# The last value block of two FFN parts, computed by feature instead of by token

## The chip, the core and the metric

The kernel runs on one core of a Trainium2 chip. The metric is device time in microseconds, the median over runs. An extra profiled execution leaves the trace from which every row here is quoted. Engines: PE does matmuls and PEld loads their stationary operand; DVE and ACT do elementwise work; POOL and SP here mostly issue DMAs, POOL the accumulating ones. Each engine works off its own queue in order.

## The reference

One layer of a hybrid decoder over 256 tokens of width 2048, in float32. The change lies in its last stage, the gated FFN with a causal convolution of three taps along the tokens, of inner width 5632:

```python
def conv_gated_ffn(hn, w_up, conv_w, conv_b, w_down):
    up = causal_dwconv(hn @ w_up, conv_w, conv_b)
    gate, val = jnp.split(up, 2, axis=-1)
    return (jax.nn.silu(gate) * val) @ w_down
```

`hn` is the normalised residual stream; the FFN's output is added to that stream, and a final normalisation follows.

## The kernel before

**Weights.** All weights stream through once, in 1 MiB pieces of 4 x 128 rows by 512 columns (`raw`, six buffers). For each piece ACT casts a high part (`hi`, L286) and DVE subtracts for a low part (`lo`, L287); there are three buffers of each. A matrix product in float32 accuracy is three products: high x high, low x high, high x low. A piece is a *unit* of PE work. The stream is prepared two units ahead, and the cast of a unit waits until PE has read the `hi` of the unit three before.

**FFN parts.** The 11 blocks of 512 inner columns are done in parts of 4, 4 and 3. In a part each block has a gate product and a value product with `ffn_w_up`, 22 in all, each of four units; then the part is multiplied by its rows of `ffn_w_down` into the residual.

**Two forms of an up product.** `gemm_n` (L362, L363 with the high part of the weights, L369 with the low part) computes *by token*: tokens on the partitions, 512 features along the free axis, one accumulator in PSUM. The convolution and the later products want features on the partitions, so the result is turned: `row_planes` splits the words into 16-bit planes (two ACT copies, L757, which also free the accumulator), `turn_planes` turns them with two transposing DMAs on SP (L1205, tile `d`), and after a number of units `join_planes` puts the words together again (four ACT copies, L763, tile `jp`), followed by a product on DVE with the tokens' scale `rsb` (L1271). `gemm_t` (L351) computes *by feature*: the weights are stationary, features come out on the partitions in two accumulators, the high part of the weights moving 512 columns and the low part 256. `scaled` then joins each accumulator's two halves (ACT copy L544, tile `c`; DVE addition L545, tile `uz`, which frees the accumulator) and multiplies by `rsb` (L676). There are three accumulators of this kind in all (`acc`).

Both forms end in `conv` (ACT L1281, DVE L1283, into `fg` for gate and `fv` for value) and, for a value block, `hidden`: a tanh (L1354), two products (L1355, L1356, tile `fo`), and a split into high and low part (L555, L556, tile `s`), once for each half `pr` of the block. Eight such `s` make `hid` of a part of four.

```python
def up(c0, b, at, then):
    if at is None:
        for pr, a in enumerate(gemm_t("ffn_w_up", 0, h2s, NT, c0 + b * BW)):
            then(pr, scaled(a, "uz"))
        return
    d = turn_planes(row_planes(gemm_n("ffn_w_up", 0, h2s, NT, c0 + b * BW)))
    def turned(pr):
        z = join_planes(d, pr)
        dve.tensor_tensor(out=z, in0=z, in1=rsb2, op=ALU.mult)
        then(pr, z)
    for pr in range(2):
        later(at[pr], lambda pr=pr: turned(pr))
```

`later(n, fn)` runs `fn` n + 1 units on in the program's text. A scheduler then orders each engine's queue from that text; the work of one step may be spread between others.

**The down pair.** In a part of four, `pair_add` computes two output blocks at a time with fewer products, in eleven units in this order: q1, p0, q3, p1, q5, q2, q6, p2, q7, q4, p3. A q unit is 12 matmuls, a p unit 24. Three weight pieces are held: A (of q1), B (of q3) and C (of q2). After q1, POOL's DMA adds a further piece onto A in SBUF (L267); that sum is q5. Then DVE adds B to A (L294) for q6, POOL's DMA adds a piece onto B for q7, and DVE adds C to A (L292) for q4. So q7 and q4 depend on a chain: q5's cast and remainder, A+=B, the accumulating DMA onto B (it may only start when B has been read), and the casts. Units p2 and p3 use the last two blocks' `hid`; p2 reads the two halves of the last value block in its matmuls (`s`). The pair takes three accumulators: q1 writes the first, p0 is the first to write the third, which p2 completes. Additions into the residual are L427.

In part 3, which has three blocks, the last value block goes by feature already (`at` is None), and its down products are plain `gemm_n`.

Of the kernel before, what the change touches and what calls it, by code (L numbers as in the profile page):

```python
# [20 lines left out]
NT = D // P  # L21
# [5 lines left out]
FF = 5632  # L27
NF = FF // P
BW = 512
# [125 lines left out]
def hybrid_layer(  # L155
# [34 lines left out]
    def big(shape, dt=F32, s="b"):  # L190
        return bp.tile(shape, dt, tag="big", name=nm(s))
# [4 lines left out]
    def acc():  # L196
        return pm.tile([P, 2, BW], F32, tag="acc", name=nm("acc"))
# [106 lines left out]
    def later(n, fn):  # L304

        pending.append((step[0] + n + 1, fn))
# [16 lines left out]
    def chunks(nk, w, row, c):  # L323

        for i, (kind, parts) in enumerate(units(w, row, nk, c)):
            yield i * KC, parts

    def gemm_t(w, row, st, nk, col):

        accs = [acc(), acc()]  # L330
        first = gemms[0] == 0
        phase = 0
        for k0, parts in chunks(nk, w, row, col):
            last = k0 + KC >= nk
            tiles = [(kk, j) for j in range(2) for kk in range(KC)]
            if first and k0 == 0:
                runs = [[(t, pr, kk, j) for t in (0, 1)] for pr in range(2) for kk in range(KC) for j in range(2)]
            elif last:
                runs = [[(t, pr, kk, j) for kk, j in tiles] for pr in range(2) for t in (1 - pr, pr)]
            else:  # L340
                runs = [[(t, pr, kk, j) for pr in range(2) for kk, j in tiles] for t in (phase, 1 - phase)]
                phase = 1 - phase
            for i, run in enumerate(runs):
                for t, pr, kk, j in run:
                    k = k0 + kk
                    sx = st[k // 2][:, k % 2, :]
                    part = parts[kk // KH][t][:, kk % KH, (2 * pr + j) * P : (2 * pr + j + 1) * P]
                    a = accs[pr][:, j, :]
                    if t == 1:
                        a, sx = a[:, S:BW], sx[:, 0:S]  # L350
                    pe.matmul(  # L351
                        a, part, sx, start=k == 0 and t == 0, stop=k == nk - 1 and t == 0, skip_group_check=True
                    )
                if i + 1 == len(runs) // 2 and not last:
                    st[(k0 + KC) // 2 + 1]
        return accs
# [14 lines left out]
    def gemm_n(w, row, st, nk, col):  # L371

        a = acc()
        for k0, parts in chunks(nk, w, row, col):
            ops = [
                [halves(st[(k0 + k) // 2], (k0 + k) % 2, slice(tt * P, (tt + 1) * P)) for k in range(KC)]
                for tt in range(2)
            ]
            for tt in range(2):
                upper_n(a[:, tt, :], ops[tt], parts, k0 == 0)  # L380
            for tt in range(2):
                lower_n(a[:, tt, :], ops[tt], parts, k0 + KC >= nk)
        return a
# [155 lines left out]
    def joined(a, s="j"):  # L539

        c = tmp("c")
        o = tmp(s)
        with tc.high_priority(URGENT):
            act.copy(c, a[:, :, S:BW])  # L544
            dve.tensor_tensor(out=o, in0=a[:, :, 0:S], in1=c, op=ALU.add)  # L545
        return o
# [127 lines left out]
    def scaled(a, s):  # L674
        z = joined(a, s)
        dve.tensor_tensor(out=z, in0=z, in1=rsb2, op=ALU.mult)  # L676
        return z
# [81 lines left out]
    def join_planes(d, pr):  # L759

        t = tmp("jp")
        for i in range(2):
            ins = act.copy(words(t)[:, :, :, 1 - i], d[:, i, 2 * pr : 2 * pr + 2, :])  # L763
            if i == 0:
                tc.keep_in_program_order(ins)
        return t
# [115 lines left out]
    for g in range(2):  # L882
        dec = big([P, 4, S], s="dec")
        vs, turned = [], []
        for b, o in enumerate((O_Q, O_K)):
            a = qjoin if g == b == 0 else [joined(t, "q") for t in gemm_t("w_in", 0, xs, NT, o + g * BW)]
# [298 lines left out]
    def row_planes(o):  # L1185

        t = big([P, 2, 2, BW], U16, s="rp")
        planes(t, o)
        return t
# [11 lines left out]
    def turn_planes(rows):  # L1201

        d = big([P, 2, KC, S], U16, s="d")
        for tt in range(2):
            sp.dma_start_transpose(  # L1205
                out=d.rearrange("p a c s -> p (a c) s")[:, :, tt * P : (tt + 1) * P],
                in_=rows[:, tt].rearrange("p a w -> p (a w)"),
            )
        return d
# [45 lines left out]
    h2s = []  # L1255
# [5 lines left out]
# [16 lines that stand above are left out]
    def conv(c0, b, pr, z, dst):  # L1277
        for j in range(2):
            t = c0 // P + 4 * b + 2 * pr + j
            y = dst[:, 2 * pr + j, :]  # L1280
            act.activation(y, z[:, j, :], AF.Identity, scale=pf[:, 2, t : t + 1], bias=pf[:, 3, t : t + 1])  # L1281
            for s in range(1, 3):
                dve.scalar_tensor_tensor(  # L1283
                    out=y[:, s:S], in0=z[:, j, 0 : S - s], scalar=pf[:, 2 - s, t : t + 1], in1=y[:, s:S],
                    op0=ALU.mult, op1=ALU.add,
                )
# [55 lines left out]
    def put_rows(n, bs):  # L1342
        for b in bs:
            sp.dma_start(out=fkept[n, b], in_=hrow[b])

    def get_rows(n, bs):
        for b in bs:
            hrow[b] = big([P, 2, BW], s="nat")
            sp.dma_start(out=hrow[b], in_=fkept[n, b])

    def hidden(gt, vl, pr, summed):
        cs = slice(2 * pr, 2 * pr + 2)
        th, o = tmp("ft"), tmp("fo")
        act.activation(th, gt[:, cs, :], AF.Tanh, scale=0.5)  # L1354
        dve.scalar_tensor_tensor(out=o, in0=th, scalar=1.0, in1=gt[:, cs, :], op0=ALU.add, op1=ALU.mult)  # L1355
        dve.tensor_tensor(out=o, in0=o, in1=vl[:, cs, :], op=ALU.mult)  # L1356
        hid.append(split_pair(o, 0.5))
        if summed and len(hid_sums) < KC:
            hid_sums.append(sums(o, 0.5))
# [3 lines left out]
    for part, nb_ in enumerate(FF_PARTS):  # L1363
        final = part == len(FF_PARTS) - 1
        paired = nb_ == 4
        hid, hid_sums = [], []
        for b in range(b0, b0 + nb_):
            gt, vl = big([P, 4, S], s="fg"), big([P, 4, S], s="fv")
            last = b + 1 == b0 + nb_
            up(0, b, (1, 2), lambda pr, z, b=b, gt=gt: conv(0, b, pr, z, gt))  # L1370
            if last:
                later(0, lambda part=part, n=2 if paired else 4: get_rows(part % 2, range(n)))

            def finish_up(pr, z, b=b, gt=gt, vl=vl, paired=paired):
                conv(FF, b, pr, z, vl)
                hidden(gt, vl, pr, paired)

            up(FF, b, None if last and not paired else (2, 4) if last else (1, 2), finish_up)
        if final:
            wfin = []  # L1380
            for i in range(2):
                t = big([P, 2, BW], s="wf")
                sp.dma_start(
                    out=t.rearrange("p a n -> p (a n)"),
                    in_=final_norm_w[i * 1024 : (i + 1) * 1024].partition_broadcast(P),
                )
                wfin.append(t)
        if nb_ == 4:
            for b in (0, 2):
                if b == 0:  # L1390
                    later(8, lambda part=part: get_rows(part % 2, (2, 3)))
                pair_add("ffn_w_down", b0 * BW, hid, hid_sums, b * BW, (b + 1) * BW, hrow[b], hrow[b + 1])
                put_rows((part + 1) % 2, (b, b + 1))
        else:
            for b in range(4):
                down(b0, hid, b, final)
        b0 += nb_
# [35 lines left out]
```

## Time and profile before

| | us |
|---|---|
| median of 3 runs (1996.22 to 1998.04) | 1997.41 |
| the profiled execution | 1995.6 |
| its span, first to last instruction | 1993.8 |
| PE busy | 1968.6 |
| DVE busy | 1566.4 |
| ACT busy | 1277.2 |

A row of the timeline reads: start, duration, engine, line, operation, output<-input, shape, count, and in brackets the idle time before it with what ended it. Line numbers are those of the kernel before. Matmuls overlap by design: two that are back to back start 0.227 us apart though each is listed with 0.39.

### The profile page before, as it was taken

The numbers are of one execution on the slowest core, as the hardware profiler recorded it, in microseconds if no ns is written. First come the engines' busy times: TensorE is split into PE (matmuls) and PEld (weight loads), VectorE is DVE, ScalarE is ACT, GpSimd is POOL, SyncE is SP. The second block draws the span as 40 slices with busy tenths as digits, with TensorE's granted clock in tenths as the row PEclk, the third lists the DMA queues.
The fourth block names the chain that finished last, engine by engine and source line by source line (L and its number), as shares of the span: only waits on it lengthen the run. The fifth ranks groups of instructions, "written<-read, shape, count | busy, mean of one in ns | idle before, by whom it ended". The sixth has DMA issues, their size and how long they took to land.

```text
span 1993.8 us, 23634 instructions
## 1 busy us (share of the span) xinstructions
PE 1968.6 (99%) x9304; PEld 1650.8 (83%) x9304; DVE 1566.4 (79%) x1546; ACT 1277.2 (64%) x1323; POOL 43.2 (2%) x52
## 2 busy tenths in 40 slices
PE   9999999999999999999999999999989999899998
PEld 7888888888888888888888888888878888788887
DVE  6978888889886886779988778677786777885775
ACT  6655656767677554567778756567744667546662
POOL 0000000000000000000000000000000000000000
PEclk9999999999999999999999999999999999899999
DMA  9675674655887865878998748766777677686671
GB/s 369 233 261 147 223 264 161 230 190 160 266 260 220 248 250 190 252 256 258 270 259 235 267 125 271 236 226 204 234 232 273 207 219 236 204 278 228 211 245 61
DMA packets 146463, 456.59 MB, mean 229 GB/s; under 512 B 77744, under 2 KB 82480, under 8 KB 98608
## 3 DMA queue, kind: packets, MB, share of 16 engines
q1 hardware_dynamic: 139072, 410.51, 58.7%
q0 software_dynamic: 5760, 41.95, 11.6%
q10 hardware_dynamic: 1520, 2.63, 0.4%
q8 instruction: 73, 1.20, 0.2%
q14 instruction: 38, 0.31, 0.0%
HBM read 420.96 MB, written 16.78 MB: 220 GB/s over the span
## 4 chain that ended last, share of the span: by engine, by line
PE 91%; DVE 4%; ACT 2%; DMA 1%; issue 1%; SPq 0%; POOLq 0%; ACTq 0%; DVEq 0%
PE acc L362 25%; PE acc L363 25%; PE acc L369 24%; PE acc L351 14%; PE sm L518 2%; DVE lo L287 1%; ACT hi L286 1%; DMA raw<-in_wall 1%; PE acc L518 1%; PE sm L948 1%; PE sm L532 1%; DVE raw L294 0%; DVE fv L1283 0%; DMA d<-rp 0%; DVE tb L722 0%
## 5 line engine op out<-in xcount | busy, mean ns | idle before, releaser
L287 DVE TENSOR_TENSOR lo<-raw,hi 128x2048 fp32r<-128x2048 f32 (+1 forms) x420 | 950.9, 2267 | 297.8 <-ACT hi L286 297.0
L286 ACT CAST hi<-raw 128x2048 fp32r<-128x2048 f32 (+1 forms) x418 | 793.2, 1901 | 522.7 <-PE acc L363 374.8
L362 PE MATMUL acc<-hi,s 128*128 128x512 f32 x2008 | 787.3, 392 | 12.4 <-ACT hi L286 12.3
L363 PE MATMUL acc<-hi,s 128*128 128x512 f32 x2008 | 784.3, 391 | 0.0
L369 PE MATMUL acc<-lo,s 128*128 128x512 f32 x2008 | 501.1, 389 | 0.0
L362 PEld LDWEIGHTS acc<-hi,s 128*128 128x128 f32 x2008 | 378.6, 189 | 91.5 <-ACT hi L286 13.2
L363 PEld LDWEIGHTS acc<-hi,s 128*128 128x128 f32 x2008 | 378.9, 189 | 78.5 <-DVE s L556 1.0
L369 PEld LDWEIGHTS acc<-lo,s 128*128 128x128 f32 x2008 | 377.1, 188 | 78.3
L351 PE MATMUL acc<-s,hi 128*128 128x512 f32 x832 | 200.4, 392 | 2.1 <-DVE hi L284 1.5
L351 PEld LDWEIGHTS acc<-s,hi 128*128 128x128 f32 x832 | 153.5, 188 | 32.8 <-issue 1.6
L362 PE MATMUL acc<-hi,ss 128*128 128x512 f32 x320 | 125.8, 393 | 0.8 <-ACT o L454 0.6
L363 PE MATMUL acc<-hi,ss 128*128 128x512 f32 x320 | 124.7, 390 | 0.0
L763 ACT COPY jp<-d 128x512 uint16<-128x512 uint16 x132 | 93.4, 771 | 29.4 <-DMA d<-rp 29.3
L351 PEld LDWEIGHTS acc<-s,lo 128*128 128x128 f32 x832 | 107.1, 191 | 4.9 <-DVE lo L287 1.3
L351 PE MATMUL acc<-s,lo 128*128 128x256 f32 x832 | 110.5, 284 | 0.5 <-DVE lo L287 0.5
L369 PE MATMUL acc<-lo,ss 128*128 128x512 f32 x320 | 85.6, 389 | 0.0
L362 PEld LDWEIGHTS acc<-hi,ss 128*128 128x128 f32 x320 | 60.1, 188 | 14.5 <-ACT o L454 1.4
L369 PEld LDWEIGHTS acc<-lo,ss 128*128 128x128 f32 x320 | 60.1, 188 | 12.6
L363 PEld LDWEIGHTS acc<-hi,ss 128*128 128x128 f32 x320 | 60.1, 188 | 12.2
L267 POOL DMA_DIRECT2D raw<-in_wall x40 | 35.2, 880 | 1550.7 <-DVE lo L287 887.5
L427 DVE TENSOR_TENSOR nat<-nat,acc 128x512 f32<-128x512 f32 (+1 forms) x49 | 44.0, 910 | 14.9 <-PE acc L369 14.9
L292 DVE TENSOR_TENSOR raw<-raw,raw 128x2048 f32<-128x2048 f32 x20 | 45.8, 2288 | 0.4
(235 smaller groups left out, 1251.7 us busy)
## 6 DMA issues: line engine op xcount, KB each, us to landing
raw<-in_wall SPq DMA_DIRECT2D x333, 1024.0 KB, 5.0
raw<-in_wall POOLq DMA_DIRECT2D x40, 1024.0 KB, 8.2
fkept<-nat SPq DMA_DIRECT2D x12, 512.0 KB, 7.7
nat<-fkept SPq DMA_DIRECT2D x12, 512.0 KB, 5.6
xt<-in_x_t SPq DMA_DIRECT2D x11, 256.0 KB, 7.8
raw<-in_wall SPq DMA_DIRECT2D x5, 512.0 KB, 7.9
nat<-in_x ACTq DMA_DIRECT2D x4, 512.0 KB, 10.1
ret<-hr SPq DMA_DIRECT2D x4, 512.0 KB, 4.6
```

Of the source, the lines that this page charges most:

```text
L267: pool.dma_start(out=raw, in_=src, accum_op=ALU.add)
L286: act.copy(hi[:, a:b], raw[:, a:b])
L287: dve.tensor_tensor(out=lo[:, a:b], in0=raw[:, a:b], in1=hi[:, a:b].bitcast(F32), op=ALU.subtract)
L292: dve.tensor_tensor(out=to, in0=to, in1=by, op=ALU.add)
L351: pe.matmul(a, part, sx, start=k == 0 and t == 0, stop=k == nk - 1 and t == 0, skip_group_check=True)
L362: pe.matmul(o, h, hi, start=start and kk == 0, stop=False, skip_group_check=True)
L363: pe.matmul(o, l, hi, start=False, stop=False, skip_group_check=True)
L369: pe.matmul(o, h, lo, start=False, stop=stop and kk == KC - 1, skip_group_check=True)
L427: dve.tensor_tensor(out=o, in0=o, in1=i, op=op)
L518: ins = pe.matmul(o, a, b, start=start and i == 0, stop=stop and i == 2, skip_group_check=True)
L532: ins = pe.transpose(t[:, j, tt * P : (tt + 1) * P], rows[:, tt, k + j * P : k + (j + 1) * P], ident)
L763: ins = act.copy(words(t)[:, :, :, 1 - i], d[:, i, 2 * pr : 2 * pr + 2, :])
```

## The change

In the two parts of four, the last value block is computed with `gemm_t` by feature; its second steps (`conv`, `hidden`) are called one and three units later instead of two and four, with the joining and scaling of the accumulators done at once. The other 19 of 22 up products stay by token, and part 3 is as it was. The amount of weights and of arithmetic is the same.

```diff
-            up(FF, b, None if last and not paired else (2, 4) if last else (1, 2), finish_up)
+            if last and paired:
+                for pr, a in enumerate(gemm_t("ffn_w_up", 0, h2s, NT, FF + b * BW)):
+                    later(1 + 2 * pr, lambda pr=pr, z=scaled(a, "uz"): finish_up(pr, z))
+            else:
+                up(FF, b, None if last else (1, 2), finish_up)
```

Three places where the queues now stand in another order follow, all of part 1; part 2 reads the same but for the buffer numbers, and elsewhere only the numbers differ.

*DVE, from q1's remainder to the first additions into the residual.* Before: `lo_10999`, `lo_11039`, `lo_11078` and `lo_11097` are the remainders of q1, p0, q3 and p1, `fg` is the last gate block, `nat` the residual.

```order
L287 TENSOR_TENSOR lo_10999<-raw_10996,hi_10998 128x2048
...
L1283 SCALAR_TENSOR_TENSOR fg_10756<-jp_11026,pf,fg_10756 128x255
L1283 SCALAR_TENSOR_TENSOR fg_10756<-jp_11026,pf,fg_10756 128x254
L287 TENSOR_TENSOR lo_11039<-raw_11036,hi_11038 128x2048
L287 TENSOR_TENSOR lo_11078<-raw_11075,hi_11077 128x2048
L427 TENSOR_TENSOR nat_10952<-nat_10952,acc_11072 128x512
L287 TENSOR_TENSOR lo_11097<-raw_11094,hi_11096 128x2048
```

Now: `lo_11016`, `lo_11064`, `lo_11115` are the remainders of q1, p0 and q3, `acc_10921` and `acc_10922` the value block's two accumulators; p0 writes into the buffer of the second.

```order
L287 TENSOR_TENSOR lo_11016<-raw_11013,hi_11015 128x2048
L1271 TENSOR_TENSOR jp_11051<-jp_11051,rsb 128x512
L287 TENSOR_TENSOR lo_11064<-raw_11061,hi_11063 128x2048
L1283 SCALAR_TENSOR_TENSOR fg_10756<-jp_11051,pf,fg_10756 128x255 x2
L1283 SCALAR_TENSOR_TENSOR fg_10756<-jp_11051,pf,fg_10756 128x254 x2
L545 TENSOR_TENSOR uz_11100<-acc_10921,c_11099 128x512
L676 TENSOR_TENSOR uz_11100<-uz_11100,rsb 128x512
L287 TENSOR_TENSOR lo_11115<-raw_11112,hi_11114 128x2048
L545 TENSOR_TENSOR uz_11105<-acc_10922,c_11104 128x512
L427 TENSOR_TENSOR nat_10961<-nat_10961,acc_11109 128x512
```

The accumulators of the value block are freed by DVE (L545) now, by ACT (L757) before; q1's remainder stands behind half of the gate block's conv steps, and q3's between the two L545.

*DVE, around the additions onto A and of the value block's second half.* Before: `raw_10996` is A, `raw_11160` C, `lo_11245` q7's remainder, `fv_10757<-jp_11206` the second half's conv, `s_11221` its low part.

```order
L1283 SCALAR_TENSOR_TENSOR fv_10757<-jp_11206,pf,fv_10757 128x255 x2
L1283 SCALAR_TENSOR_TENSOR fv_10757<-jp_11206,pf,fv_10757 128x254 x2
L292 TENSOR_TENSOR raw_10996<-raw_10996,raw_11160 128x2048
L1356 TENSOR_TENSOR fo_11217<-fo_11217,fv_10757 128x512
L287 TENSOR_TENSOR lo_11245<-raw_11075,hi_11244 128x2048
L556 SCALAR_TENSOR_TENSOR s_11221<-fo_11217,s_11221 128x2x256
```

Now: A is `raw_11013`, C is `raw_11193`, q7's remainder `lo_11274`, the second half's conv `fv_10757<-uz_11105`, its low part `s_11234`.

```order
L1283 SCALAR_TENSOR_TENSOR fv_10757<-uz_11105,pf,fv_10757 128x255 x2
L1283 SCALAR_TENSOR_TENSOR fv_10757<-uz_11105,pf,fv_10757 128x254 x2
L1355 SCALAR_TENSOR_TENSOR fo_11230<-ft_11229,fg_10756 128x512
L287 TENSOR_TENSOR lo_11238<-raw_11013,hi_11237 128x2048
L1356 TENSOR_TENSOR fo_11230<-fo_11230,fv_10757 128x512
L287 TENSOR_TENSOR lo_11256<-raw_11253,hi_11255 128x2048
L556 SCALAR_TENSOR_TENSOR s_11234<-fo_11230,s_11234 128x2x256
L292 TENSOR_TENSOR raw_11013<-raw_11013,raw_11193 128x2048
L287 TENSOR_TENSOR lo_11274<-raw_11112,hi_11273 128x2048
```

The conv of the second half moved up from just ahead of A+=C (L292) to behind q2's remainder; its low part moved from behind q7's remainder to ahead of A+=C.

*PE, from p2's first matmuls.* Before: p2 writes `acc_11074` with `hi_11226`; `s_11157` and `s_11221` are the halves of the last value block; `acc_11073<-hi_11261` is q4.

```order
L362 MATMUL acc_11074<-hi_11226,s_11157 128x512
L363 MATMUL acc_11074<-hi_11226,s_11157 128x512
L362 MATMUL acc_11073<-hi_11261,s_10178 128x512
L362 MATMUL acc_11074<-hi_11226,s_11221 128x512
L363 MATMUL acc_11073<-hi_11261,s_10178 128x512
L363 MATMUL acc_11074<-hi_11226,s_11221 128x512
L362 MATMUL acc_11074<-hi_11226,s_11221 128x512
L363 MATMUL acc_11074<-hi_11226,s_11221 128x512
```

Now: p2 is `acc_11111` with `hi_11255` and the halves `s_11172` and `s_11234`; `acc_11110<-hi_11290` is q4, `acc_11109<-hi_11273` q7.

```order
L362 MATMUL acc_11111<-hi_11255,s_11234 128x512
L363 MATMUL acc_11111<-hi_11255,s_11234 128x512
L369 MATMUL acc_11111<-lo_11256,s_11172 128x512 x2
L369 MATMUL acc_11111<-lo_11256,s_11234 128x512 x2
L369 MATMUL acc_11111<-lo_11256,s_11172 128x512 x2
L369 MATMUL acc_11111<-lo_11256,s_11234 128x512 x2
L362 MATMUL acc_11110<-hi_11290,s_10178 128x512
L363 MATMUL acc_11110<-hi_11290,s_10178 128x512
L362 MATMUL acc_11109<-hi_11273,ss_10181 128x512
L363 MATMUL acc_11109<-hi_11273,ss_10181 128x512
```

Two matmuls of q4 moved from the middle of p2 to behind it; they stay ahead of q7.

## The prediction

> **What bounds the kernel now.** I read the page first, then who waited on PE, then busy time in stretches around the two places where a wait shows, then PE's timeline and the chain of waits there.
>
> ```profile
> span 1993.8 us, 23634 instructions
> PE 1968.6 (99%) x9304; PEld 1650.8 (83%) x9304; DVE 1566.4 (79%) x1546; ACT 1277.2 (64%) x1323; POOL 43.2 (2%) x52
> PE acc L362 <- ACT hi L286: 12.3, 2, 6.3
> PE acc L351 <- DVE hi L284: 1.5, 1, 1.5
> ```
>
> The span is 1993.8 us and PE covers 99% of it, so the time is PE's matmuls plus the few places where PE waits. The last two lines are the head of PE's list of waits (us in total, times, longest): two waits for a weight cast make up 12.3 us, one of them 6.3; the next is 1.5, and no other reaches that. The next rows say where they lie (us; PE, PEld, DVE, ACT, POOL busy; granted clock; DMA share; GB/s).
>
> ```profile
> 1410.42:1432.18 21.76, 21.76 (x98) 18.02 (x96) 14.73 (x16) 14.64 (x16) 0.90 (x1) 1.00 0.95 261
> 1432.18:1456.66 24.48, 24.48 (x110) 20.28 (x108) 20.53 (x18) 17.93 (x18) 0.89 (x1) 1.00 0.57 148
> 1456.66:1471.06 14.40, 8.34 (x27) 6.08 (x26) 11.19 (x11) 5.58 (x6) 0.00 (x0) 0.76 0.76 296
> 1500.00:1680.00 180.00, 180.00 (x796) 149.08 (x795) 132.76 (x141) 117.64 (x114) 0.00 (x0) 1.00 0.71 233
> 1720.85:1736.35 15.50, 9.22 (x27) 6.68 (x26) 11.50 (x11) 5.84 (x6) 0.00 (x0) 0.67 0.76 302
> 1896.39:1918.61 22.22, 22.22 (x129) 19.68 (x128) 13.92 (x15) 14.63 (x18) 0.00 (x0) 1.00 0.87 289
> ```
>
> Row 1 is the last value block of part 1, by token: four units in 21.76 us, so 5.44 for a unit of 24 matmuls and 0.227 a matmul. Row 2 is the first seven units of the down pair behind it (q1, p0, q3, p1, q5, q2, q6): five of 2.72 and two of 5.44, no wait. Row 3 runs from the first matmul of p2 to the first of q7: 14.40 us for 24 matmuls of p2 and two of q4, which are worth 5.89. Row 5 is the same place of part 2: 15.50. **So part 1 loses 8.51 us there and part 2 loses 9.61: 18.12 in all.** Between them (row 4) PE is never idle; whatever is saved in rows 3 and 5 therefore comes off the span, and nothing later takes it back.
>
> ```profile
> 1457.34 0.39 PE L363 MATMUL acc<-hi,s 128*128 128x512 f32 x1
> 1463.79 1.33 PE L362 MATMUL acc<-hi,s 128*128 128x512 f32 x2 [6.07 <-ACT hi L286]
> 1466.23 0.63 PE L363 MATMUL acc<-hi,s 128*128 128x512 f32 x1
> 1466.66 0.63 PE L362 MATMUL acc<-hi,s 128*128 128x512 f32 x1
> ```
>
> PE stops after p2's fourth matmul and resumes 6.4 us later; then the starts are 0.43 apart instead of 0.227, at the lowered clock that rows 3 and 5 show in their mean (0.76, 0.67). The chain of waits tells what it stood for:
>
> ```profile
> 1435.61 3.14 DMA d<-rp
> 1439.47 1.91 ACT hi L286
> 1441.40 2.29 DVE lo L287
> 1444.21 2.30 DVE raw L294
> 1447.15 8.09 DMA raw<-in_wall
> 1455.34 1.92 ACT hi L286
> 1457.26 0.51 ACT fv L1281
> 1458.28 1.27 DVE fv L1283 x3
> 1459.55 2.21 DVE raw L292
> 1461.84 1.91 ACT hi L286
> ```
>
> From the top: the transposes of the last value block; the cast and remainder of q5; A+=B (L294); the accumulating DMA onto B, 8.09 us; the cast of q7; then the value block's second half on ACT (`fv`) and DVE; only behind it A+=C (L292), and the cast of q4 at 1461.84. PE's order makes p2 wait for that cast.
>
> The rows shown with the change are the place: before, PE holds two matmuls of q4 (`hi_11261`) in the middle of p2. Now all of p2 stands ahead of q4's two matmuls, which still stand ahead of q7. So the same cast has 4.5 us more before PE wants it.
>
> **The change part by part.** Part 2 has the same order as part 1, and outside these two places the orders differ in names only. Times below are of part 1, in the trace's clock.
>
> *The block itself.* Part 3 ends in a block by feature today: row 6, 22.22 us against 21.76. Two blocks: **+0.92 us**. This form loads weights 32 times a unit instead of 24, and in row 6 loads are busy 19.68 of 22.22 us beside the matmuls, which never stop: covered. The Trainium skill (TensorE: Matmul & The Clock Gate, section "LDWEIGHTS (loading the stationary operand)") gives a load its columns over 1.2, so 107 ns for 128; if the 64 extra loads were not covered that would be 6.8 us more, an estimate from that page, and the trace's row 6 speaks against it.
>
> *Removed beside PE.* Two plane copies and four joins on ACT, two transposes on SP, a block; SP's weight loads behind them go out earlier, into a stream that made PE wait nowhere in row 4, so that is worth nothing. None is PE time. They matter by what they held up: the transposes' landing held ACT, and with it q5's cast at 1439.47. But PE frees that cast's buffer only after p0's uppers (the 16 matmuls with the high parts of the weights, 3.63 us), at 1432.18 + 2.72 + 3.63 = 1438.53, so this alone is worth under 1 us. The real gain is that the conv of the second half goes to ACT and DVE before the accumulating DMA lands, not after.
>
> *Added: PSUM.* The block now fills two of three accumulators, and p0's first matmul needs the second back. It comes free at the second L545 on DVE.
>
> The rows of DVE's queue shown with the change have, from q1's remainder on: the product with `rsb` for the gate block's second half, p0's remainder, four conv steps, L545 and L676 of the first half, q3's remainder, and only then the second L545. So a whole queue stands ahead of the release, and q1's cast has slipped behind the gate block's joins on ACT. When do these start? The gate block's two transposes in part 1 and in part 2 with their times to landing, and the durations:
>
> ```profile
> L1205 SPq DMA_TRANSPOSE d<-rp x2: 1244/2653/4062, 1413.6 to 1414.9; - x2
> DMA to landing us min/median/max: 6.2/6.4/6.6
> L1205 SPq DMA_TRANSPOSE d<-rp x2: 1232/2458/3684, 1677.8 to 1679.1; - x2
> DMA to landing us min/median/max: 5.7/5.9/6.1
> 1421.55 2.67 ACT L763 COPY jp<-d 128x512 uint16<-128x512 uint16 x4
> 1424.60 2.08 ACT L1281 ACTIVATE fg<-jp,pf 128x256 f32<-128x256 f32 x4 [0.39 <-DVE jp L1271]
> 1426.59 1.90 ACT L286 CAST hi<-raw 128x2048 fp32r<-128x2048 f32 x1
> 1423.88 1.29 DVE L1271 TENSOR_TENSOR jp<-jp,rsb 128x512 f32<-128x512 f32 x2
> 1425.24 3.49 DVE L1283 SCALAR_TENSOR_TENSOR fg<-jp,pf,fg 128x255 f32<-128x255 f32 x8
> 1428.65 2.28 DVE L287 TENSOR_TENSOR lo<-raw,hi 128x2048 fp32r<-128x2048 f32 x1
> 1918.74 0.68 DVE L545 TENSOR_TENSOR uz<-acc,c 128x512 f32<-128x512 f32 x1
> 1924.32 0.68 DVE L545 TENSOR_TENSOR uz<-acc,c 128x512 f32<-128x512 f32 x1
> ```
>
> They land by 1414.9 + 6.2 = 1421.1. Two joins to 1422.5, the product with `rsb` to 1423.1, two conv starts on ACT to 1424.3, q1's cast to 1426.2. DVE then: q1's remainder to 1428.4, `rsb` 1429.0, p0's remainder 1431.2, four conv steps 1432.9, L545 1433.5, L676 1434.1, q3's remainder 1436.3, L545 1437.0. The block ends at 1432.18 + 0.46 = 1432.64 and p0 is due 2.72 later, at 1435.36: PE waits 1.7 us. In part 2 they land at 1679.1 + 5.7 = 1684.8, which is 11.6 before that block's end today (1720.85 - 24.48 = 1696.37), against 11.1 in part 1; so 0.5 less: 1.2. **+2.9 us.** Nothing of before shows this wait, so its ends: none, if DVE's steps run closer; and as in part 3 today, where the second L545 is over 6.4 us after the block's end (1925.0 against 1918.61), so 3.7 a part. I take my own queue, since every duration in it is a row. Behind that first matmul stands all of PE's work. On ACT the copies `c` are new waits for PE, with q3's cast behind the first and p1's behind the second; PE fills the first accumulator 2.7 us (12 matmuls' worth) before the block's end and the second at it, and q3 is due 2.72 + 5.44 = 8.2 after it, p1 still later: covered by p0; without that cover a cast of 1.9 us would come on top.
>
> *The old wait.* p0 then starts at 1437.0 and its uppers end 3.63 later; q5's cast runs 1440.9 to 1442.8, remainder to 1445.0, a product 1445.6, A+=B to 1447.8, and the accumulate goes out 0.64 later as before, at 1448.45. It lands 8.1 later, 1456.55. q7's cast to 1458.5, the half's high part on ACT (0.6) and low part on DVE (0.65) to 1459.75: p2, which starts at 1432.64 + 24.48 + 1.7 = 1458.8, wants it five matmuls in, 1459.95. A+=C to 1461.95, q4's cast to 1463.9, wanted at 1458.8 + 5.44 = 1464.25. Both just in time; I put **0.4 us** for two parts. Cover is thin: if the accumulate lands later by x, PE waits x - 0.3.
>
> ```profile
> DMA to landing us min/median/max: 7.9/8.2/11.8
> ```
>
> That is all 40 accumulates: the middle is safe, the slowest is not. The first accumulate, onto A, goes out at 1428.9 and even at 11.8 lands before q5's cast can run.
>
> *Sum.* -18.12 + 0.92 + 2.9 + 0.4 = -13.9 us on the profiled execution's 1995.6: 1981.7. The median of the runs lies 1.8 above that execution (1997.4), so **1983.5 us**.
>
> *The clock.* In part 1 PE idles from 1457.57 to 1463.79, 6.2 of the 8.51, so 2.3 went at the lowered clock; in part 2, whose wait is 0.2 longer by the list, 3.2 of 9.61. PE's list has no wait between 1.5 and 6 us, so the trace does not show where the drop begins. The Trainium skill (same page, "What's actually happening") puts the drop behind one idle window of about 3.4 us: by that rule the 1.7 above costs nothing more, a wait of 3.7 would.
>
> **The rivals.** A, 17%: p0 does not wait, because DVE's queue is shorter than I lined up (conv steps and products interleave): -18.12 + 0.92 + 0.4, so 1980.6. For it: DVE is busy only 14.73 of 21.76 us in row 1.
>
> B, 12%: the release comes as late as in part 3's rows, 3.7 us a part: 1988.0, and 1993.5 if the clock falls as it does after the 6 us waits (2.3 to 3.2 a part). Against it: there DVE does the gate's work after the block.
>
> C, 12%: the accumulate lands at its slowest, 3.7 us later than its middle: 1983.5 + 2 x 3.4 = 1990.3. Against it: 8.09 in the chain at this very place.
>
> D, 4%, slower: one mechanism, the new release of the accumulator, so late that PE idles into the lowered clock in both parts. With 2.75 us of clock each (the middle of 2.3 and 3.2), it eats the 16.8 us at a wait of 5.65 us; past 7.65 us the kernel is slower by 0.2%. At 8.5 us: 2003.1. It needs L545 11 us after the block's end, where my queue has 4.4.
>
> E, 3%: the change moves the wait but does not shorten it, as q4's two matmuls still stand ahead of q7: the 18.12 stay, plus 0.92, so 1998.3, no change.
>
> **How the numbers follow.** My forecast has 52%, with its own range 1981 to 1986. A lies just below, so the low end is 1979.5 (A, less the 1.2 by which the fastest run of before lies under the median); the high end 1990.5 takes in C and the half of B that keeps the clock. Left out are B's other half, D, E and some of the edges, under 20%. A measurement of this kernel can tell 0.2%, 4 us, from no change. Faster by more: forecast, A, B, C, 93%; within: E, 3%; slower: D, 4%.
>
> **What would show it.** Right: a by-feature block of 22.2 us at both places, L545's second step 4 to 5 us after it, one wait of 1 to 2 us before p0 on DVE's L545, p2 to q7 in about 6 us at clock 1.00, and no other wait. Wrong: p0 without a wait (A), the clock under 1.00 behind the block (B, D), or PE still waiting some us for a cast inside p2 or ahead of q7 (C, E).

## The result, and the profile after

The changed kernel takes 1984.18 us in the median (1982.25 to 1986.44, 4 runs) against 1997.09 (1996.22 to 1998.04): ratio 0.9935, 95% interval 0.9923 to 0.9948, so some 13 us or 0.65% less, clear of the noise. The forecast was 1983.5. Measured once more beside the experiments, it took 1982.88 (0.9933, 0.9920 to 0.9945). Both of its profiled executions are used: the first, of 1986.44 us, is the slowest of its four; the second, of 1982.26, the fastest of its five.

The head of the page and of PE's list of waits, first profile of the changed kernel:

```profile
span 1984.6 us, 23752 instructions
PE 1968.9 (99%) x9368; PEld 1653.5 (83%) x9368; DVE 1568.1 (79%) x1550; ACT 1271.2 (64%) x1315; POOL 43.2 (2%) x52
PE acc L362 <- ACT s L555: 2.1, 3, 1.5
PE sm L518 <- DVE s L553: 1.6, 1, 1.6
```

PE does 64 more matmuls (a unit by feature has 32, a unit by token 24), and its two long waits for a cast are gone from the list. What leads it now is a wait for `s` of L555, the high part of a half of `hid`. The second wait, 1.6 us near 1058 us, is not put down to the change: it stands 350 us ahead of the changed places, and the second profile of the same kernel has none. Waits of 1 to 2 us between 1040 and 1060 us come and go in these profiles; the one of before had none.

By stretches: before from p2's first matmul to p3's, in parts 1 and 2, and the changed kernel from the value block to p3, part 1 and then part 2.

```profile
1456.66:1476.05 19.39, 13.32 (x49) 10.21 (x48) 15.97 (x16) 8.51 (x8) 0.00 (x0) 0.82 0.73 277
1720.85:1741.35 20.50, 14.22 (x49) 10.81 (x48) 16.30 (x16) 8.72 (x8) 0.00 (x0) 0.75 0.68 261
```

```profile
1413.22:1435.44 22.22, 22.22 (x130) 19.68 (x129) 14.77 (x17) 14.47 (x17) 0.90 (x1) 1.00 0.75 223
1435.44:1459.94 24.50, 24.50 (x110) 20.28 (x109) 24.47 (x26) 14.90 (x14) 0.89 (x1) 1.00 0.68 183
1459.94:1474.75 14.81, 13.05 (x49) 10.06 (x48) 12.50 (x10) 8.88 (x6) 0.00 (x0) 0.88 0.82 312
1673.31:1695.53 22.22, 22.22 (x130) 19.68 (x128) 14.87 (x17) 14.45 (x17) 0.86 (x1) 1.00 0.74 226
1695.53:1720.04 24.51, 24.51 (x111) 20.29 (x110) 24.48 (x25) 16.01 (x15) 0.89 (x1) 1.00 0.66 186
1720.04:1732.26 12.22, 11.69 (x49) 8.85 (x48) 11.02 (x8) 7.67 (x6) 0.00 (x0) 1.00 0.86 327
```

Blocks of 22.22 us, as priced. Then seven units in 24.5 us, no wait before p0, though DVE is busy in all of that stretch. The last row of each part is p2, q7 and q4: 48 matmuls, worth 48 x 0.2267 = 10.88 us. That gives one number per place, the **loss** from p2 to p3: before 8.51 and 9.62, now 3.93 and 1.34. The second profile has 1.92 and 1.47:

```profile
1457.94:1470.74 12.80, 11.69 (x49) 8.85 (x48) 11.02 (x8) 8.25 (x6) 0.00 (x0) 1.00 0.82 312
1716.03:1728.38 12.35, 11.70 (x50) 8.85 (x48) 11.03 (x8) 7.79 (x6) 0.00 (x0) 1.00 0.87 323
```

The books close: 1995.6 - 18.13 + 0.92 + 3.39 (+ 0.06 ahead of p2) = 1981.8 for the second profile, which took 1982.26. The first gives 1983.7, and 1985.3 with its 1.6 us near 1058; it took 1986.44.

What p2 still waits for, in the chain of waits and on PE's timeline of the first profile:

```profile
1450.87 9.09 DMA raw<-in_wall
1460.06 1.90 ACT hi L286
1461.96 0.54 ACT s L555
1462.52 0.70 DVE s L556
```

```profile
1460.62 0.39 PE L363 MATMUL acc<-hi,s 128*128 128x512 f32 x1
1462.54 0.50 PE L362 MATMUL acc<-hi,s 128*128 128x512 f32 x1 [1.53 <-ACT s L555]
1463.27 0.55 PE L363 MATMUL acc<-hi,s 128*128 128x512 f32 x1 [0.23 <-DVE s L556]
1463.62 0.63 PE L362 MATMUL acc<-hi,s 128*128 128x512 f32 x1
1464.04 0.63 PE L363 MATMUL acc<-hi,s 128*128 128x512 f32 x1
```

p2 stops after its fourth matmul for the second half's `s`. That step stands on ACT behind q7's cast, and the cast behind the accumulating DMA. So the accumulate still reaches PE, through ACT's queue and not through its data.

### The profile page after: what moved, and what is told of

The parts are those of the page before. It is cut to its first block, busy times and chain, and to the rows that moved or that the text cites. A ratio compares the mean times of both kernels' runs of the same rounds, so it can differ in the third digit from the quotient of the medians.

```text
span 1984.6 us, 23752 instructions
## 1 busy us (share of the span) xinstructions
PE 1968.9 (99%) x9368; PEld 1653.5 (83%) x9368; DVE 1568.1 (79%) x1550; ACT 1271.2 (64%) x1315; POOL 43.2 (2%) x52
## 4 chain that ended last, share of the span: by engine, by line
PE 90%; DVE 4%; issue 2%; DMA 2%; ACT 1%; SPq 0%; POOLq 0%; ACTq 0%; DVEq 0%
PE acc L369 24%; PE acc L362 24%; PE acc L363 24%; PE acc L351 15%; PE sm L518 2%; DVE lo L287 2%; DMA raw<-in_wall 2%; ACT hi L286 1%; PE acc L518 1%; PE sm L948 1%; PE sm L532 1%; DVE raw L294 0%; DVE fv L1283 0%; DVE tb L722 0%; SPq L1205 0%
## 5 line engine op out<-in xcount | busy, mean ns | idle before, releaser
L362 PE MATMUL acc<-hi,s 128*128 128x512 f32 x1944 | 760.1, 391 | 2.1 <-ACT s L555 2.1
L363 PE MATMUL acc<-hi,s 128*128 128x512 f32 x1944 | 758.0, 390 | 0.4 <-DVE s L556 0.4
L369 PE MATMUL acc<-lo,s 128*128 128x512 f32 x1944 | 485.2, 389 | 0.0
L362 PEld LDWEIGHTS acc<-hi,s 128*128 128x128 f32 x1944 | 365.5, 188 | 78.0 <-ACT s L555 3.3
L363 PEld LDWEIGHTS acc<-hi,s 128*128 128x128 f32 x1944 | 365.7, 188 | 76.2 <-DVE s L556 1.3
L369 PEld LDWEIGHTS acc<-lo,s 128*128 128x128 f32 x1944 | 364.9, 188 | 75.8
L351 PE MATMUL acc<-s,hi 128*128 128x512 f32 x960 | 232.1, 393 | 0.9 <-DVE hi L284 0.9
L351 PEld LDWEIGHTS acc<-s,hi 128*128 128x128 f32 x960 | 178.0, 189 | 36.8 <-issue 1.1
L351 PEld LDWEIGHTS acc<-s,lo 128*128 128x128 f32 x960 | 123.9, 192 | 5.2 <-DVE lo L287 1.1
L351 PE MATMUL acc<-s,lo 128*128 128x256 f32 x960 | 127.2, 284 | 0.5 <-DVE lo L287 0.5
L763 ACT COPY jp<-d 128x512 uint16<-128x512 uint16 x124 | 87.9, 772 | 35.0 <-DMA d<-rp 34.8
L427 DVE TENSOR_TENSOR nat<-nat,acc 128x512 f32<-128x512 f32 (+1 forms) x49 | 44.0, 910 | 6.0 <-PE acc L369 6.0
L292 DVE TENSOR_TENSOR raw<-raw,raw 128x2048 f32<-128x2048 f32 x20 | 45.8, 2289 | 0.4
```

The source lines that it names most:

```text
L292: dve.tensor_tensor(out=to, in0=to, in1=by, op=ALU.add)
L351: pe.matmul(a, part, sx, start=k == 0 and t == 0, stop=k == nk - 1 and t == 0, skip_group_check=True)
L362: pe.matmul(o, h, hi, start=start and kk == 0, stop=False, skip_group_check=True)
L363: pe.matmul(o, l, hi, start=False, stop=False, skip_group_check=True)
L369: pe.matmul(o, h, lo, start=False, stop=stop and kk == KC - 1, skip_group_check=True)
L427: dve.tensor_tensor(out=o, in0=o, in1=i, op=op)
```

## The experiments

In each kernel one time tells most: when the second half's `s` is complete (end of L556), counted from the end of the value block, in part 1. PE, when it does not wait, wants it 25.4 us after the block (24.5 for seven units, 0.9 for four matmuls). All times in us; "ahead" is what both parts lose between the block and p2, beyond 24.48 each.

| kernel | median | `s` ready | ahead | p2 to p3, part 1 + 2 |
|---|---|---|---|---|
| before | 1997.1 | 33.0 | 0 | 8.51 + 9.62 |
| before, q6 urgent | 1996.3 | 33.4 | 0 | 8.60 + 8.08 |
| by token, steps 1 and 3 | 1994.3 | 30.5 | 1.75 | 7.46 + 6.58 |
| changed in part 1 alone | 1991.0 | 27.9 | 0.03 | 4.02 + 8.01 |
| by token, joined early | 1988.3 | 27.9 | 2.75 | 2.72 + 2.67 |
| the same, q6 urgent | 1985.4 | 28.0 | 5.13 | 1.39 + 0.40 |
| by feature, steps 2 and 4 | 1985.5 | 27.5 | 0.06 | 2.06 + 3.70 |
| by feature, steps at once | 1984.7 | 18.6 | 0.20 | 1.69 + 1.59 |
| accumulators exchanged | 1983.4 | 27.8 | 0.06 | 2.61 + 1.36 |
| **the change**, second time | 1982.9 | 27.1 | 0.06 | 1.92 + 1.47 |
| by feature, at once, q6 urgent | **1979.2** | 18.4 | 0.20 | 0 + 0 |

**The change again.** No edit.

> The changed kernel once more, so that the others are compared with it on one chip. Its first profile was of its slowest run (1986.4; median 1984.2). If the 4.2 us that part 1 still lost in p2 there came from an accumulating DMA that landed 1.1 us later than the middle, this profile should lose less in p2 (1 to 2 us a part, as part 2 did, and no lowered clock) and the median should lie at 1982 to 1986 either way. If the loss is built into the order of ACT's queue, it is there again: some 4 us in part 1.

Measured 1982.88 (1982.26 to 1986.19). Part 1 loses 1.92 with the accumulate landing 8.57 us after its issue, against 3.93 with 9.09. So a wait of 1 to 2 us a part is built in, and its size varies with the landing and, as told below, with the clock.

**By token, second steps one unit earlier.**

```diff
-            up(FF, b, None if last and not paired else (2, 4) if last else (1, 2), finish_up)
+            up(FF, b, None if last and not paired else (1, 3) if last else (1, 2), finish_up)
```

> The last value blocks stay by token as before; only their second steps come one unit earlier, after one and three units instead of two and four, as in the changed kernel. Theory T (timing: the gain is that the second half's conv no longer stands behind the wait for the accumulating DMA, and q4 no longer inside p2): most of the gain without the other form: 1982 to 1988, with a value block of 21.76 us; the half's high part `s` still stands behind q7's cast, so p2 still loses 1 to 4 us a part. Rival F (form: the gain is that the transposes' landing no longer holds ACT ahead of q5's cast, so that the whole chain of additions starts earlier): q5's cast as late as before, so 1993 to 1998.

Measured 1994.31 (0.9983, 0.9974 to 0.9992): the number of rival F. F's condition holds too: q5's cast starts 8.45 us after the block (1442.23 - 1433.78), before 7.29 (1439.47 - 1432.18). But the gain of the changed kernel cannot hang on that chain, as its A+=B starts no sooner either: 12.5 us after the block (1447.94 - 1435.44), before 12.0 (1444.21 - 1432.18). The trace names another reason. The transposes had landed by 1440.44, when ACT began the joins. On DVE's timeline of this kernel, the second half's product with `rsb`, conv, L1356, A+=C and low part:

```profile
1453.56 0.69 DVE L1271 TENSOR_TENSOR jp<-jp,rsb 128x512 f32<-128x512 f32 x1
1456.96 1.66 DVE L1283 SCALAR_TENSOR_TENSOR fv<-jp,pf,fv 128x255 f32<-128x255 f32 x4
1460.74 0.69 DVE L1356 TENSOR_TENSOR fo<-fo,fv 128x512 f32<-128x512 f32 x1
1461.34 2.29 DVE L292 TENSOR_TENSOR raw<-raw,raw 128x2048 f32<-128x2048 f32 x1
1463.54 0.69 DVE L556 SCALAR_TENSOR_TENSOR s<-fo,s 128x512 fp32r<-128x512 f32 x1
```

From the landing to the product of the second half 13 us pass: its joins are called only after three units, and each step behind them queues behind casts, remainders and additions. That argued for place rather than form, and called for a block by token whose joins come early. Theory T's number failed as well, and with it a part of its reason: the conv now stands ahead of the landing (1450.88 + 8.07 = 1458.95), and yet only 2 to 3 us are gained, for the steps behind it are still late. PE's timeline shows what p2 waits for here:

```profile
1462.14 0.50 PE L362 MATMUL acc<-hi,s 128*128 128x512 f32 x1 [2.82 <-ACT s L555]
1464.29 0.79 PE L363 MATMUL acc<-hi,s 128*128 128x512 f32 x1 [1.64 <-DVE s L556]
```

These are p2's own operands; no matmul of q4 stands in the way, and part 1 loses 7.46 us all the same.

**By feature, second steps as late as before.** The delay `1 + 2 * pr` becomes `2 + 2 * pr`.

> By feature as in the changed kernel, but the second steps after two and four units as the blocks by token had them. Theory T (timing): the second half's conv goes back behind the accumulating DMA's landing and A+=C ahead of the half's low part: p2 loses 2 to 6 us a part again, 1988 to 1996. Rival F (form): the gain stays, 1983 to 1986, since q5's cast is as early as in the changed kernel.

Measured 1985.50 (0.9940, 0.9927 to 0.9952): only 1 to 3 us worse than the change, so theory T's number fails and rival F's holds. With the scaled values there early, ACT's part of the second conv runs where it ran in the changed kernel, just ahead of q5's cast. DVE's part slid by 2.1 us (1454.58, 19.6 us after the block, for 17.5) and still ran ahead of the landing; the low part slid behind A+=C (3.70 lost in part 2). So this kernel did not put the second half back where before had it, and it could not tell form from place; the next one can.

**By token, joined early, and q6 urgent.** The block stays by token; both halves are joined and scaled after one unit. Against the changed kernel; the second place stands further up in the file:

```diff
-                for pr, a in enumerate(gemm_t("ffn_w_up", 0, h2s, NT, FF + b * BW)):
-                    later(1 + 2 * pr, lambda pr=pr, z=scaled(a, "uz"): finish_up(pr, z))
+                d = turn_planes(row_planes(gemm_n("ffn_w_up", 0, h2s, NT, FF + b * BW)))
+
+                def joined_early(d=d, finish_up=finish_up):
+                    zs = [join_planes(d, pr) for pr in range(2)]
+                    for z in zs:
+                        dve.tensor_tensor(out=z, in0=z, in1=rsb2, op=ALU.mult)
+                    finish_up(0, zs[0])
+                    later(1, lambda: finish_up(1, zs[1]))
+
+                later(1, joined_early)
...
-            with tc.high_priority(URGENT):
+            with tc.high_priority(4 * URGENT if kind == "q6" and w == "ffn_w_down" else URGENT):
```

> The last value blocks by token, but with both halves joined and scaled after one unit, the first half's conv and hidden at once behind that and the second half's one unit on; and q6's subtraction from the residual gets more urgency, which puts it on DVE ahead of q7's remainder. So the form is that of before, and the place in DVE's and ACT's queues that of the changed kernel: the second half's high part stands ahead of q7's cast, its low part ahead of A+=C. Theory P (place: the time was lost because the second half's joins, scaling and conv stood late, behind casts and the accumulating DMA's landing): the whole gain without the other form, 0.92 us less for two value blocks, 1980 to 1985. Theory F (form: the transposes land some 6 us behind the block, and that alone makes the chain too late): 1989 to 1995, as the blocks by token with steps after one and three units gave 1994.3.

Measured 1985.43 (0.9941, 0.9929 to 0.9954), just above theory P's range. Rival F falls: nearly the whole gain comes without the other form. What the form costs shows ahead of p2. From q1 to p2 and from p2 to p3, part 2:

```profile
1690.78:1719.22 28.44, 26.32 (x109) 21.34 (x108) 23.18 (x23) 18.05 (x20) 0.89 (x1) 0.94 0.53 118
1719.22:1730.50 11.28, 11.18 (x50) 8.93 (x49) 10.63 (x8) 8.05 (x5) 0.00 (x0) 1.00 1.00 371
```

PE loses 3.96 us before p2, 2.1 of it in one wait for q6's cast and the rest mostly at the lowered clock behind it (mean 0.94). The cast is late since A+=B is: it starts 17.9 us after the block in part 1 (1450.37 - 1432.48), against 12.5 in the changed kernel. Ahead of it q5's cast waited for the landing and the four joins on ACT, and ran 10.7 us after the block (1443.19 - 1432.48), against 6.6 (1442.05 - 1435.44). Ahead of p2 that costs 5.13 for both parts here; the block by feature costs 0.92.

**The same without the urgency.**

> The block by token with early joins, without the urgency for q6; PE then has four matmuls of q4 ahead of q7. Theory P: nearly as with the urgency (1985.4), plus what q7 or q4 wait for behind p2, 0 to 3 us: 1985 to 1989. If the urgency was what made the block by token fast: 1992 to 1995, as the blocks by token with steps after one and three units.

Only the first part of that edit. Measured 1988.29 (0.9957, 0.9944 to 0.9969): theory P again. The early joins do nearly all of it. The medians put the urgency at 3 us, the two intervals overlap, and the losses in the table differ by 1.2 (8.14 for 6.92), so its worth to this kernel is 1 to 3 us.

**Before, with the urgency alone.**

> The kernel before with only q6's subtraction from the residual made more urgent. PE's order then has matmuls of q7 inside p2, where before has two of q4; ACT's order is as before, so the second half's high part still stands behind q4's cast. Theory P (place: the late second half is what p2 waits for, q4's two matmuls only stood in the same place): p2 still stops for that high part; about 1 us a part is filled by q7's matmuls, 1993 to 1997. Rival O (order on PE: the stop was that q4 stood inside p2): most of the gain, 1982 to 1988. As a control of the fastest kernel: if the urgency alone gave its 18 us, 1979 to 1982.

Measured 1996.25 (0.9995, 0.9986 to 1.0004): no change. PE's timeline, and ACT's:

```profile
1466.14 0.77 PE L362 MATMUL acc<-hi,ss 128*128 128x512 f32 x1 [5.22 <-DVE nat L427]
1464.89 1.90 ACT L286 CAST hi<-raw 128x2048 fp32r<-128x2048 f32 x1 [3.60 <-DVE raw L292]
1466.69 0.63 ACT L555 ACTIVATE s<-fo 128x512 fp32r<-128x512 f32 x1
```

Now q7's matmul stands in p2's middle, and waits for q6's subtraction (L427) on DVE. But the `s` that p2 needs next runs at 1466.69 all the same. By itself this is no clean proof against rival O, as one stop in PE's queue was exchanged for another. The block by token with steps after one and three units is: no matmul of q4 stands at p2's stop there, and p2 waits for `s` itself and loses 7.46 us. The late half is late by itself.

**By feature, all steps at once.** Against the kernel before:

```diff
-            up(FF, b, None if last and not paired else (2, 4) if last else (1, 2), finish_up)
+            up(FF, b, None if last else (1, 2), finish_up)
```

> By feature, with conv and hidden of both halves called at once instead of one and three units later. The half's high part `s` then stands far ahead of q7's cast on ACT. Theory S (what p2 still lost, 4.2 and 1.3 us in the changed kernel's profile, is that `s` stands behind q7's cast and with it behind the accumulating DMA): both losses go, p2 to q7 takes 5.9 us in both parts, 1978 to 1981. Rival Q (the early conv and hidden steps, some 8 us of DVE and 5 of ACT, push back the remainders and casts of q1, p0 and q3): PE waits there instead, 1 to 4 us a part, 1984 to 1990.

Measured 1984.66 (0.9934, 0.9921 to 0.9946). Theory S had the mechanism right, `s` is ready at 18.6 and p2 runs through, but not the sum: a new wait took the place, ahead of q7. The number is rival Q's, but not by its mechanism, as both parts lose only 0.20 ahead of p2. PE, and the two rows of DVE behind it:

```profile
1467.54 0.47 PE L362 MATMUL acc<-hi,ss 128*128 128x512 f32 x1 [1.44 <-DVE nat L427]
1464.51 2.29 DVE L287 TENSOR_TENSOR lo<-raw,hi 128x2048 fp32r<-128x2048 f32 x1 [1.20 <-ACT hi L286]
1466.71 0.68 DVE L427 TENSOR_TENSOR nat<-nat,acc 128x512 f32<-128x512 f32 x1
```

q7 writes where q6's result lay. Its subtraction from the residual stood on DVE behind q7's own remainder, though q6's last matmul had ended at 1460.66.

**The same with q6 urgent.** The urgency line from above.

> By feature with conv and hidden at once, as in the kernel that lost 1.6 and 1.5 us ahead of q7, where DVE's subtraction of q6 from the residual stood behind q7's remainder; that subtraction now gets more urgency and stands ahead of it. If that is what held q7: 1980 to 1982, no wait over 0.4 us from q1 to p3 in either part. If the late landing of the accumulating DMA (2 us behind p2's start there) holds q7 then instead, with its cast and remainder: 1983 to 1985, a wait for q7's cast or remainder of about 1 us a part.

Measured 1979.17 (1978.38 to 1980.25; 0.9907, 0.9892 to 0.9923), the fastest, and a little under the range that was expected. From p2 to p3 in parts 1 and 2, and then DVE's timeline in part 1, where the subtraction now precedes q7's remainder:

```profile
1457.34:1468.22 10.88, 10.88 (x49) 9.01 (x48) 10.37 (x7) 8.16 (x5) 0.00 (x0) 1.00 0.92 329
1713.63:1724.51 10.88, 10.88 (x50) 9.01 (x48) 10.24 (x7) 8.05 (x5) 0.00 (x0) 1.00 0.95 327
```

```profile
1459.98 0.68 DVE L427 TENSOR_TENSOR nat<-nat,acc 128x512 f32<-128x512 f32 x1
1461.16 4.49 DVE L287 TENSOR_TENSOR lo<-raw,hi 128x2048 fp32r<-128x2048 f32 x2 [0.51 <-ACT hi L286]
```

Both places lose nothing. Here the accumulate goes out 18.5 us after the block (the change: 15.4) and lands 1.8 us after p2's start, and PE does not notice, because only casts, q7's first, stand behind it on ACT; the second half's `s` was done long before (18.4).

**Part 1 alone.** The condition `last and paired and part == 0`.

> The change in part 1 alone; part 2 keeps the block by token with steps after two and four units. If the two places are independent: about half of the gain, 1988.5 to 1992, with part 2's place at 15.5 us from p2 to q7 as before. If part 1's later work moves part 2's (a common cause), nearer to one of the two ends.

Measured 1990.95 (0.9968, 0.9956 to 0.9981): half of the gain, the places are independent within a us or two (part 1 loses 4.02 as in the change, part 2 8.01 for 9.62).

**Accumulators exchanged.** `xz, rw, yu = acc(), acc(), acc()`.

> The changed kernel with the second and third accumulator of every pair handed out in exchanged order, and nothing else. In the changed kernel p0 started on time though the value block's second addition that frees an accumulator ran 0.8 us after p0's start; so p0 must have taken the one freed by the first. Theory A1: exchanged, p0 takes the other, and the wait that I had predicted appears: 1.2 to 1.7 us a part before p0 for DVE's second addition. As p2 waits 1 to 2 us for the half's high part anyway, and that part's chain does not go through p0, the wait inside p2 shrinks by as much, and the time stays at 1982 to 1986. Theory A2: that wait comes on top, 1985.5 to 1987. Rival: no wait before p0, since the order in which accumulators are asked for does not set the buffer: as the changed kernel in every row.

Measured 1983.41 (0.9928, 0.9914 to 0.9941); the rival: p0 starts on time again. On PE and DVE:

```profile
1437.26 0.39 PE L362 MATMUL acc<-hi,s 128*128 128x512 f32 x1
1437.94 0.69 DVE L545 TENSOR_TENSOR uz<-acc,c 128x512 f32<-128x512 f32 x1
```

There are three accumulators: the gate block's is taken by q1, and the second of the value block is not free yet when p0 starts. So in both kernels p0 writes where the block's *first* accumulator was, and exchanging the order of asking did not alter that. The kernel in which p0 takes the other was not made, so the price of that wait stays unmeasured.

## Why the prediction was right, and where not

**The places and the 18.12 us: right.** Nothing later took the gain back, and the sum of losses gives every kernel's profiled time within 2.2 us, once the wait near 1050 us is added where it occurs.

**The block, +0.92: right,** 22.22 us twice. The 64 extra loads stay covered (19.68 us of loads beside matmuls that never stop in those stretches).

**p0's wait, +2.9: wrong; it was 0.** The step that failed is "p0's first matmul needs the second back" (and with it the words beside DVE's order, that p0 writes into the second's buffer). DVE's queue was lined up well: the second L545 was put 4.4 us after the block's end, and came 4.2 after it (1439.63). But p0 had started at 1438.18:

```profile
1438.18 0.39 PE L362 MATMUL acc<-hi,s 128*128 128x512 f32 x1
1438.95 0.68 DVE L545 TENSOR_TENSOR uz<-acc,c 128x512 f32<-128x512 f32 x1
```

**The old wait, +0.4: wrong; it was 5.27 and 3.39** (both parts, first and second profile). The prediction led the chain to the second `s` by p0: PE frees the buffer of q5's cast only after p0's uppers, so p0's 1.7 us of waiting put off the cast and all that follows, and the half was to be complete 27.11 us after its block (1459.75), just in time for a p2 put off by the same 1.7. With p0 on time, q5's cast did run 1.7 us sooner, 6.6 us after the block for 8.3. But its remainder did not follow at once. ACT's and DVE's timelines of the first profile, with the second half's conv as the last row:

```profile
1442.05 1.92 ACT L286 CAST hi<-raw 128x2048 fp32r<-128x2048 f32 x1
1442.95 1.66 DVE L1283 SCALAR_TENSOR_TENSOR fv<-uz,pf,fv 128x255 f32<-128x255 f32 x4
1445.13 2.28 DVE L287 TENSOR_TENSOR lo<-raw,hi 128x2048 fp32r<-128x2048 f32 x1
1452.94 1.66 DVE L1283 SCALAR_TENSOR_TENSOR fv<-uz,pf,fv 128x255 f32<-128x255 f32 x4
```

The cast ended at 1443.97 and the remainder started at 1445.13, behind the first half's conv and product on DVE: 1.2 us that the prediction had put at nothing. The accumulate then took 9.09 and 8.57 us instead of 8.1. So `s` was complete after 27.77 and, in the second profile, 27.13 us (1460.56 - 1433.43), as late as forecast for a kernel with a wait at p0, while PE came to p2 1.7 us earlier and waited there.

That 27.13 meets 27.11 is luck, and so is a good part of the forecast: the terms for p0 and for p2 were both wrong, and their sum of 3.3 stood against 3.45 and 5.32 measured. By the prediction's own signs, p0 without a wait and a wait inside p2 speak against it. Rival A had p0 right, though not its reason (DVE's queue was as long as lined up), and was too fast by the wait in p2. "If the accumulate lands later by x, PE waits x - 0.3" held in direction, and through ACT's queue: between the two profiles the landing of part 1 differs by 0.52 us and PE's wait for `s` by 0.64.

**The real gain** was named as "the conv of the second half goes to ACT and DVE before the accumulating DMA lands". That step is in the traces: before, the conv starts on ACT at 1457.26, behind the landing at 1455.24; now the last row above starts at 1452.94, ahead of the landing at 1459.96. But it is not the whole of it, since by token with steps after one and three units the conv is ahead of the landing as well and little is gained. What the losses follow is the time of `s`, set by all of its steps. The accumulate itself does not go out sooner: 15.0 us after the block before (1447.15 - 1432.18), 15.4 now (1450.87 - 1435.44). `s` comes 5 to 6 us sooner, 33.0 to 27.8 and 27.1. By token with early joins it comes at 28, with nearly the same time. The form itself is a means: it has the values in place without landing and joins.

**The clock: wrong.** By the rule of the Trainium skill that the prediction took (TensorE: Matmul & The Clock Gate, "What's actually happening"), a wait of 1.7 us was to cost nothing more. In the first profile the waits of 1.53 and 0.23 us were followed by matmuls 0.43 apart and a mean clock of 0.88 over that stretch; that is about 1.6 us of its 3.93 (8 matmuls, 0.2 each). In the second profile the waits were shorter, 0.89 us the longest, and the mean clock was 1.00.

## What to carry to other kernels

Count from the producer, not along the engine that waits: a wait taken away upstream on PE does not shorten a chain that another queue holds up just as long; it only shows further on. A short step that feeds the bound engine should not stand, in an in-order queue, behind one that waits for a DMA; look for the last small step (a split, a subtraction that frees an accumulator) and move that ahead. And a change of form may be worth only the places it gives to steps: try the places alone.

## What the hardware showed that was not expected

The drop of the clock had no fixed length of wait here. After 1.53 and 0.23 us the changed kernel ran its next 8 matmuls 0.43 us apart; after waits of the same size the one with exchanged accumulators did not. Its PE timeline, and its stretch from p2 to p3 at a mean clock of 1.00:

```profile
1461.64 0.50 PE L362 MATMUL acc<-hi,s 128*128 128x512 f32 x1 [1.56 <-ACT s L555]
1462.37 0.50 PE L363 MATMUL acc<-hi,s 128*128 128x512 f32 x1 [0.22 <-DVE s L556]
```

```profile
1459.02:1472.51 13.49, 11.71 (x49) 8.85 (x48) 11.08 (x8) 8.76 (x6) 0.00 (x0) 1.00 0.78 299
```

The Trainium skill (TensorE: Matmul & The Clock Gate, "What's actually happening") lets a free-running window of about 3.4 us decide, idle for the lower clock. That the same wait ends either way agrees with a window that does not start with the wait; that 1.8 us of waiting can be enough does not agree with a whole idle window of 3.4.

The accumulating DMAs of 1 MiB took 7.8 to 9.2 us from issue to landing at this place in all profiles (median of all 40 in the changed kernel's first profile 8.2), beside other transfers.
